# Channel mixer of a hybrid decoder layer on one core: the value sums and gelu's output are kept in PSUM, and the transposes of h are spread over the out projection

## The chip, the cores and the metric

The kernel runs on one core of a Trainium2 chip. The metric is the device time of one execution in microseconds (us). The engines are named as in the profile: PE is TensorE (PEld its weight loads), DVE is VectorE, ACT is ScalarE, POOL is GpSimd, SP is the queue that issues the DMAs. Each engine works through its own queue in order. SBUF is the on-chip memory that all engines read; PSUM is the accumulator memory that PE writes, eight banks of 512 fp32 for each of 128 partitions.

## The reference, cut to what matters

One decoder layer on x of 512 rows and 1024 columns. The change touches the second part of it only, from the out projection to the channel mixer:

```python
x = x + y @ w_out[i]
hf = rmsnorm(x, norm_ffn[i])
up = causal_dwconv(hf @ w_up[i], ffn_dw_w[i], ffn_dw_b[i])   # width 3, per channel
gate, val = jnp.split(up, 2, axis=-1)                        # 2816 channels each
x = x + (jax.nn.gelu(gate) * val) @ w_down[i]
```

Before it stand the conformer and attention mixers, behind it a gated per-layer embedding (`w_ple_gate`, `w_ple`) and a last norm.

## The kernel before, in words

**Numbers in two parts.** Every fp32 operand of a product is cut in two: a rounded high part, written by ACT (`hi_of`, L117), and the remainder, a subtraction (`lo_of`, L120) on DVE, for some blocks on POOL. A product is then three matmuls (high by high, high by low, low by high).

**Pairs.** The up projection and gelu run over 22 pairs f: 128 gate channels and the 128 value channels that belong to them. The rows are two halves of 256, the inner dimension two halves of 512, and each pair is made by a scheme of seven block products instead of eight (Strassen's kind). A product (`mm_block`, L133) is four inner blocks by three matmuls of 128x256, so a pair is 84 matmuls. They are called m1 to m7 and use sums of weight blocks: block 11 (m1, m2), t12 (m5, m6), t34 (m7, m4) and 22 (m3). Two PSUM banks take gates and two take values, in turn by f; LO and HI are a bank's halves. The products build on each other through ACT copies: m1 goes to an extra bank, is copied to the value bank's HI (L1322) and from there to the gate bank's LO (L1325); value HI is copied to value LO after m6 (L1336) and to gate HI after m7 (L1345); m5 is copied to SBUF (L1331).

**The stream of weights.** `Stream` (L218) keeps one list, `pieces`. A piece is loaded by SP, summed on POOL (an "add": two subtractions of 128x512, L307; "a" gives t12, "b" gives t34), or cut into hi and lo. `pump` cuts the next pieces as far as free buffers allow (four buffers `whl`; `done` frees one) and issues the next DMAs; `work` issues the pending lo part. For each pair DVE cuts 11, t12 and t34 (128x1024 each), POOL cuts 22 (128x512) and makes the four subtractions.

**The tail of a pair.** `after` (L1361) is a generator of steps: DVE adds m5 to the value bank into an SBUF tile v (L1366); ACT makes the middle tap and the bias of gate and value (L1371, L1373); DVE adds the other two taps (L1359: ug reads the gate bank, uv reads v); ACT makes gelu in SBUF (L1376); DVE multiplies (L1379); then hi and lo of the activations.

**The order.** It is written out by hand. `slot` (L1445) issues a product, the pending lo part, one step of each tail, then a pump. In the steady state the slots of a turn are m6, m2 of f, m1 of f+1, m7 of f, m5 of f+1, m3, m4 of f. After pairs 7 and 14 the down projection of the earlier pairs is put in (168 matmuls of 128x512), behind m1.

**The out projection** (`rows_product`, L1188 on) takes the row tiles t in the order 0, 2, 1, 3 in its second half. In the middle of a tile, after three of the four weight pieces (i == 2), `out_late` transposes the normed rows of the tile before: for tile 2 the sums s1, s2; for tile 1 its own halves and then s3, s4 and a22 of tile 2. `before_last` (L1412) does the norm of tile 3, the first half of the embedding's product, and m1 of pairs 0 and 1.

Of the kernel before, what the change touches and what calls it, by code (L numbers as in the profile page):

```python
# [12 lines left out]
AF = mybir.ActivationFunctionType  # L13
# [3 lines left out]
P = 128  # L17
# [66 lines left out]
def block_kernel(ctx: ExitStack, tc: tile.TileContext, x, p, rel_bias, norm_mix, w_in, conv_dw_w, conv_dw_b,  # L84
# [103 lines left out]
    def up_sums(*names):  # L188
        for name, f in names:
            pieces.append(((name, f), None, 4 if name == "22" else KC, P, "add" if name in ("a", "b") else "sum"))  # L190
# [4 lines left out]
    up_raw(0)  # L195
    up_sums(("a", 0), ("b", 0))
    up_raw(1)
    up_sums(("a", 1))
    ple_piece(0)
    up_sums(("11", 0), ("11", 1), ("t12", 0), ("t12", 1), ("b", 1), ("t34", 0), ("22", 0))  # L200
    for f in range(1, NF):
        if f + 1 < NF:
            up_raw(f + 1)
# [14 lines left out]
    class Stream:  # L218
# [133 lines left out]
        def done(self):  # L352
            self.hls -= 1
# [834 lines left out]
    def rows_product(name, ks, a_of, done, late=None, filler=None, between=None, last=None, banks=None, order=range(NT),  # L1188
                     cut_on=False):


        for n in range(2):
            o = [banks(n, t) if banks else ps() for t in range(NT)]

            def part(t, kk, hl):
                for j, k in enumerate(kk):
                    a_hi, a_lo = a_of(k, t)
                    mm_a(o[t], a_hi, a_lo, hl[:, 0, j, :], hl[:, 1, j, :], k == ks[0], k == ks[-1])

            hls = []  # L1200
            for i in range(0, len(ks), 2):
                kk = ks[i:i + 2]
                st.pump()
                hl = st.take(name, n, ks[i])
                hls.append((kk, hl))
                if n == 0 or late is None:
                    for t in range(NT):
                        part(t, kk, hl)
                        st.work()
                    st.done()  # L1210
            if n == 0 or late is None:
                for t in range(NT):
                    done(t, n, o[t])
                continue
            if between:
                between()
            before = None
            for t in order:
                if t == NT - 1 and last:
                    last(hls, o[t])  # L1220
                    break
                for i, (kk, hl) in enumerate(hls):
                    part(t, kk, hl)
                    st.work()
                    if t == NT - 1:
                        st.done()
                        if i < 2:
                            st.pump()
                    if cut_on and i == 2 and before is not None:
                        late(before)  # L1230
                done(t, n, o[t])
                if cut_on:
                    st.pump()
                elif before is not None:
                    late(before)
                before = t
            if filler:
                filler()
            if not last and not cut_on:
                late(NT - 1)  # L1240
# [30 lines left out]


    hf, hsum = {}, {}
    ROWS_FIRST, EVERY = ("s1", "s2"), ("s1", "s2", "s3", "s4", "a22")

    def row_sums(t):

# [35 lines left out]
    class Pair:  # L1313


        def __init__(self, f):
            self.f, self.gate, self.value, self.extra = f, gates[f % 2], values[f % 2], ps()

        def m1(self):
            self.b1 = st.take("11", self.f)  # L1320
            mm_block(self.extra[:, HI], self.b1, 0, hf["a11"], True)
            nc.scalar.activation(self.value[:, HI], self.extra[:, HI], AF.Copy)  # L1322

        def seed_gate(self):
            nc.scalar.activation(self.gate[:, LO], self.value[:, HI], AF.Copy)  # L1325

        def m5(self):
            self.t12 = st.take("t12", self.f)
            mm_block(self.extra[:, LO], self.t12, 0, hf["s1"], True)
            self.e = work("m5", (P, 256), tag="sc", bufs=2)  # L1330
            nc.scalar.activation(self.e, self.extra[:, LO], AF.Copy)  # L1331

        def m6(self):
            mm_block(self.value[:, HI], self.t12, 4, hf["s2"], False)
# [26 lines left out]
        def after(self):  # L1361

            f, c = self.f, NF + self.f
            uv, ug, v = [work(name, (P, 512), tag="S", bufs=8) for name in ("uv", "ug", "v")]
            halves = lambda a: a.rearrange("p (h t) -> p h t", h=2)
            nc.vector.tensor_tensor(halves(v), halves(self.value), self.e.unsqueeze(1).broadcast_to((P, 2, 256)),  # L1366
                                    op=ALU.add)
            yield
            yield
            yield  # L1370
            nc.scalar.activation(ug, self.gate, AF.Identity, scale=fw(2, f), bias=fw(3, f))  # L1371
            yield
            nc.scalar.activation(uv, v, AF.Identity, scale=fw(2, c), bias=fw(3, c))  # L1373
            self.taps(ug, self.gate, f)
            yield
            nc.scalar.activation(ug, ug, AF.Gelu_apprx_tanh)  # L1376
            self.taps(uv, v, c)
            yield
            nc.vector.tensor_tensor(uv, ug, uv, op=ALU.mult)  # L1379
            yield  # L1380
            a = act[f] = work("a", (P, 2, 512), F32R, tag="act", bufs=8)
            hi_of(a[:, 0], uv)
            yield
            yield
            yield
            lo_of(a[:, 1], uv, a[:, 0])
# [13 lines left out]
    def out_done(t, n, o):  # L1400
        residual(t, n, o, gain_f)
        if n and t != 3:
            ready(t)
        if n and t == 1:
            st.adds = 1

    def out_late(t):
        turn_halves(t, ROWS_FIRST if t == 2 else EVERY)
        if t == 1:
            turn_halves(2, ("s3", "s4", "a22"))  # L1410

    def before_last():  # L1412
        ready(3)
        st.adds = len(pieces)
        st.pump()
        ple_half(0)
        st.work()
        st.pump()
        pairs[0] = Pair(0)
        pairs[0].m1()  # L1420
        st.work()
        st.pump()
        turn_halves(3, ("s1",))
        pairs[0].seed_gate()
        pairs[1] = Pair(1)
        pairs[1].m1()
        st.work()
        st.pump()
        turn_halves(3, ("s2",))
        pairs[1].seed_gate()  # L1430

    rows_product("out", list(range(KC)),
# [9 lines left out]
            if next(tail, tails) is tails:  # L1442
                tails.remove(tail)

    def slot(product, cut=True):  # L1445

        product()
        st.work()
        step()
        if cut:  # L1450
            st.pump()

    def down(f0, f1, gain, *late, **kw):
        rows_product("down%d" % f0, list(range(f0, f1)),
# [7 lines left out]
    for f in range(NF):  # L1462
        this, coming = pairs[f], pairs.get(f + 1)
        if f == 0:
            slot(this.m5)
            turn_halves(3, ("s3",))
            slot(coming.m2)
            slot(this.m6)
            turn_halves(3, ("s4",))
            slot(coming.m5)  # L1470
            turn_halves(3, ("a22",))
            slot(this.m7)
            slot(this.m2)
        else:
            cut = f not in DOWN_IN
            slot(this.m6, cut)
            if f > 1:
                slot(this.m2, cut)
            else:
                step()  # L1480
            if f + 1 < NF:
                coming = pairs[f + 1] = Pair(f + 1)
                slot(coming.m1, cut)
            if f in DOWN_IN:
                step()
                st.pump(most=1)
                step()
                st.work()
                drain()
                down(*DOWN_IN[f], None, banks=lambda n, t: ps() if t < 3 else coming.gate)  # L1490
            slot(this.m7)
            if f + 1 < NF:
                slot(coming.m5)
                coming.seed_gate()
        tails.append(this.after())
        slot(this.m3)
        slot(this.m4)
    drain()
    gain_p = load_gain(norm_ple)
    hpT = [work("hpT", (P, 2, KC, P), F32R, tag="hf", bufs=7) for t in range(NT)]  # L1500
# [88 lines left out]
```

## Time and profile before

| | us |
|---|---|
| median of 3 runs (lowest, highest) | 855.8 (854.69, 857.84) |
| profiled execution, its own time | 857.31 |
| span of that execution | 855.3 |
| PE busy (share of the span) | 811.9 (95%) |
| DVE busy | 633.2 (74%) |
| ACT busy | 441.8 (52%) |
| POOL busy | 202.3 (24%) |

The span is the time from the first to the last recorded instruction; 2.0 us of the execution lie around it. Busy shares are means over stages with different limits. Matmuls overlap in the pipeline, so PE's pace is read from the distance of their starts and not from their durations. The out projection's second half and the pairs lie between 365 and 764 us of the span.

### The profile page before, as it was taken

How to read it: one execution, taken by the hardware profiler on the slowest of the kernel's cores; microseconds unless marked ns; L12 is line 12 of the kernel's file. 1: busy time of each engine (PE TensorE's matmuls, PEld its weight loads, DVE VectorE, ACT ScalarE, POOL GpSimd, SP SyncE). 2: the span in 40 equal slices, each digit the busy share in tenths (PEclk: the TensorE clock that was granted, in tenths of full speed). 3: DMA queues.
4: the chain of work that ended last, by engine and by line, in shares of the span. 5: the costliest groups of instructions: out<-in, count | busy, mean ns of one | idle time of the engine just before them, and what ended most of it. 6: DMA issues, size and time to landing. Idle time of an engine off the chain costs nothing.

```text
span 855.3 us, 12272 instructions
## 1 busy us (share of the span) xinstructions
PE 811.9 (95%) x4688; PEld 702.5 (82%) x4688; DVE 633.2 (74%) x965; ACT 441.8 (52%) x839; POOL 202.3 (24%) x183
## 2 busy tenths in 40 slices
PE   8999999999999999998898899998899998999996
PEld 6788888888888877876888898798887898888885
DVE  6479988888878879557698884388984388864664
ACT  6333434387779764335566653165662266642543
POOL 2000000000010000043585670147640256401012
PEclk9999999999999999999999999999999999999999
DMA  6347777221101122640233223313323332141322
GB/s 212 106 99 207 187 181 166 65 61 50 50 28 47 50 97 101 221 123 26 75 99 99 63 62 136 111 52 97 99 72 101 99 100 74 35 151 62 123 74 99
DMA packets 108070, 84.69 MB, mean 99 GB/s; under 512 B 4113, under 2 KB 93641, under 8 KB 108011
## 3 DMA queue, kind: packets, MB, share of 16 engines
q1 hardware_dynamic: 108010, 83.90, 33.6%
q8 instruction: 37, 0.61, 0.3%
q14 instruction: 23, 0.18, 0.1%
HBM read 79.36 MB, written 2.43 MB: 96 GB/s over the span
## 4 chain that ended last, share of the span: by engine, by line
PE 66%; DVE 24%; ACT 4%; issue 3%; POOL 1%; DMA 1%; SPq 0%; POOLq 0%; DVEq 0%; ACTq 0%
PE ps L128 9%; PE ps L130 9%; PE ps L129 8%; PE ps L142 8%; PE ps L141 8%; PE ps L143 8%; DVE whl L121 8%; DVE uv L1359 6%; DVE uv L1379 3%; ACT whl L118 3%; DVE ug L1359 3%; PE ps L869 2%; PE ps L895 2%; PE ps L675 2%; PE ps L137 1%
## 5 line engine op out<-in xcount | busy, mean ns | idle before, releaser
L121 DVE TENSOR_TENSOR whl<-wraw,whl 128x512 fp32r<-128x512 f32 (+1 forms) x140 | 130.6, 945 | 107.4 <-ACT whl L118 107.1
L137 PE MATMUL ps<-hf,whl 128*128 128x256 f32 x616 | 178.9, 290 | 12.0 <-DVE whl L121 11.3
L135 PE MATMUL ps<-hf,whl 128*128 128x256 f32 x616 | 178.4, 290 | 10.6 <-ACT whl L118 9.5
L136 PE MATMUL ps<-hf,whl 128*128 128x256 f32 x616 | 176.6, 287 | 2.0 <-DVE hf L121 2.0
L118 ACT ACTIVATE whl<-wraw 128x512 fp32r<-128x512 f32 (+1 forms) x160 | 123.5, 794 | 94.1 <-PE ps L143 43.0
L137 PEld LDWEIGHTS ps<-hf,whl 128*128 128x128 f32 x616 | 120.4, 195 | 16.1 <-DVE whl L121 15.2
L135 PEld LDWEIGHTS ps<-hf,whl 128*128 128x128 f32 x616 | 120.3, 195 | 13.3 <-ACT whl L118 11.8
L136 PEld LDWEIGHTS ps<-hf,whl 128*128 128x128 f32 x616 | 120.4, 195 | 2.3 <-DVE hf L121 2.2
L128 PE MATMUL ps<-hT,whl 128*128 128x512 f32 x256 | 101.9, 398 | 0.0
L130 PE MATMUL ps<-hT,whl 128*128 128x512 f32 x256 | 100.2, 391 | 0.3 <-DVE whl L121 0.3
L129 PE MATMUL ps<-hT,whl 128*128 128x512 f32 x256 | 99.9, 390 | 0.0
L735 DVE SCALAR_TENSOR_TENSOR acc<-aT,convw,acc 128x512 f32<-128x512 f32 x120 | 86.1, 745 | 1.0
L307 POOL TENSOR_TENSOR tt<-wraw 128x512 f32<-128x512 f32 x44 | 66.0, 1500 | 81.0 <-DVE whl L121 76.9
L307 POOL TENSOR_TENSOR tt<-wraw,tt 128x512 f32<-128x512 f32 x44 | 71.7, 1629 | 9.2 <-DVE whl L121 6.0
L121 DVE TENSOR_TENSOR whl<-tt,whl 128x1024 fp32r<-128x1024 f32 x44 | 54.9, 1278 | 23.1 <-ACT whl L118 23.1
L141 PE MATMUL ps<-whl,a 128*128 128x512 f32 x176 | 70.7, 402 | 0.6 <-DVE x L1256 0.6
L142 PE MATMUL ps<-whl,a 128*128 128x512 f32 x176 | 70.4, 400 | 0.0
L143 PE MATMUL ps<-whl,a 128*128 128x512 f32 x176 | 70.2, 399 | 0.0
L1359 DVE SCALAR_TENSOR_TENSOR uv<-v,ffnw,uv 128x511 f32<-128x511 f32 (+1 forms) x44 | 63.3, 1439 | 1.1 <-ACT uv L1373 0.3
L118 ACT ACTIVATE whl<-tt 128x1024 fp32r<-128x1024 f32 x44 | 46.0, 1046 | 22.4 <-PE ps L143 19.0
L130 PEld LDWEIGHTS ps<-hT,whl 128*128 128x128 f32 x256 | 48.1, 188 | 11.3 <-DVE whl L121 0.7
L128 PEld LDWEIGHTS ps<-hT,whl 128*128 128x128 f32 x256 | 48.1, 188 | 9.0 <-issue 0.2
(214 smaller groups left out, 1548.2 us busy)
## 6 DMA issues: line engine op xcount, KB each, us to landing
wraw<-in_w_up SPq DMA_DIRECT2D x44, 512.0 KB
wraw<-in_w_in SPq DMA_DIRECT2D x32, 512.0 KB
wraw<-in_w_down SPq DMA_DIRECT2D x20, 512.0 KB
wraw<-in_w_out SPq DMA_DIRECT2D x8, 512.0 KB
wraw<-in_w_ple_gate SPq DMA_DIRECT2D x8, 512.0 KB
W<-vdram SPq DMA_DIRECT2D x8, 264.0 KB
xin<-in_x SPq DMA_DIRECT2D x4, 512.0 KB
wraw<-in_w_ck SPq DMA_DIRECT2D x4, 512.0 KB
```

Source lines behind the costliest of these rows:

```text
L118: nc.scalar.activation(dst, src, AF.Copy, scale=scale)
L121: engine.tensor_tensor(dst, src, f32(hi), op=ALU.subtract)
L128: nc.tensor.matmul(o, hl[:, 0, j, cs], a_hi, start=start, stop=False)
L129: nc.tensor.matmul(o, hl[:, 0, j, cs], a_lo, start=False, stop=False)
L130: nc.tensor.matmul(o, hl[:, 1, j, cs], a_hi, start=False, stop=stop)
L135: nc.tensor.matmul(o, hl[:, 0, j0 + k, :], a[:, 0, k, :], start=start and k == 0, stop=False, skip_group_check=True)
L136: nc.tensor.matmul(o, hl[:, 0, j0 + k, :], a[:, 1, k, :], start=False, stop=False, skip_group_check=True)
L137: nc.tensor.matmul(o, hl[:, 1, j0 + k, :], a[:, 0, k, :], start=False, stop=k == 3, skip_group_check=True)
L141: nc.tensor.matmul(o, a_hi, w_hi, start=start, stop=False)
L142: nc.tensor.matmul(o, a_hi, w_lo, start=False, stop=False)
L143: nc.tensor.matmul(o, a_lo, w_hi, start=False, stop=stop)
L1359: nc.vector.scalar_tensor_tensor(u[:, d:], o[:, :S - d], fw(k, c), u[:, d:], op0=ALU.mult, op1=ALU.add)
```

## The change

Five things change. (1) The sum v is written back into the value bank, and both value taps and the ACT step read it there. (2) gelu's output goes to the gate bank and the product reads it there. (3) In the tail the value's ACT step and taps come before the gate's, and gelu and the product one step later each. (4) m1 and m5 take a PSUM bank each; the copies of m1 to the value and the gate bank move to the slots of m5 and m4 of the turn; m1 follows the down projection; a slot pumps before it steps the tails. (5) In the out projection the transposes are put at i == 2 or i == 3 by a table, the sum "a" of pair 1 comes later in `pieces`, and `before_last` pumps one piece only. The last down projection gets a pump and a `work` at the end of its first half.

```diff
-    up_sums(("a", 1))
     ple_piece(0)
-    up_sums(("11", 0), ("11", 1), ("t12", 0), ("t12", 1), ("b", 1), ("t34", 0), ("22", 0))
+    up_sums(("11", 0), ("11", 1), ("t12", 0), ("a", 1), ("t12", 1), ("b", 1), ("t34", 0), ("22", 0))
...
-                    if cut_on and i == 2 and before is not None:
-                        late(before)
+                    if cut_on and before is not None:
+                        late(before, i)
...
         def m1(self):
-            self.b1 = st.take("11", self.f)
-            mm_block(self.extra[:, HI], self.b1, 0, hf["a11"], True)
-            nc.scalar.activation(self.value[:, HI], self.extra[:, HI], AF.Copy)
+            self.first = ps()
+            self.b1 = self.b1 or st.take("11", self.f)
+            mm_block(self.first[:, LO], self.b1, 0, hf["a11"], True)
+
+        def seed_value(self):
+            nc.scalar.activation(self.value[:, HI], self.first[:, LO], AF.Copy)
 
         def seed_gate(self):
-            nc.scalar.activation(self.gate[:, LO], self.value[:, HI], AF.Copy)
+            nc.scalar.activation(self.gate[:, LO], self.first[:, LO], AF.Copy)
...
-            uv, ug, v = [work(name, (P, 512), tag="S", bufs=8) for name in ("uv", "ug", "v")]
+            uv, ug = [work(name, (P, 512), tag="S", bufs=8) for name in ("uv", "ug")]
+            v = self.value
...
+            nc.scalar.activation(uv, v, AF.Identity, scale=fw(2, c), bias=fw(3, c))
+            yield
             nc.scalar.activation(ug, self.gate, AF.Identity, scale=fw(2, f), bias=fw(3, f))
+            self.taps(uv, v, c)
             yield
-            nc.scalar.activation(uv, v, AF.Identity, scale=fw(2, c), bias=fw(3, c))
             self.taps(ug, self.gate, f)
             yield
-            nc.scalar.activation(ug, ug, AF.Gelu_apprx_tanh)
-            self.taps(uv, v, c)
+            nc.scalar.activation(self.gate, ug, AF.Gelu_apprx_tanh)
             yield
-            nc.vector.tensor_tensor(uv, ug, uv, op=ALU.mult)
+            nc.vector.tensor_tensor(uv, self.gate, uv, op=ALU.mult)
...
+    TURNS = {(0, 2): (0, ()), (2, 3): (2, ("s1", "s2")), (1, 2): (1, ()), (1, 3): (2, ("s3", "s4", "a22"))}
+
+    def out_late(t, i):
+        if (t, i) in TURNS:
+            turn_halves(*TURNS[t, i])
...
-    def slot(product, cut=True):
+    def slot(product, then=None, cut=True):
 
         product()
         st.work()
-        step()
+        if then:
+            then()
         if cut:
             st.pump()
+        step()
...
             if f + 1 < NF:
-                slot(coming.m5)
-                coming.seed_gate()
+                slot(coming.m5, coming.seed_value)
         tails.append(this.after())
         slot(this.m3)
-        slot(this.m4)
+        slot(this.m4, coming.seed_gate if 0 < f < NF - 1 else None)
```

## Rows read from the trace of the kernel before

**Rows 1.** The chain of waits between 597 and 635 us: shares of the stretch by engine and line, then one link of a turn (start us, length us, what).
```profile
by line: DVE whl L121 26.3%; DVE uv L1359 25.3%; DVE uv L1379 17.0%; DVE ug L1359 11.2%; ACT whl L118 11.1%; issue 7.7%; DVE a L121 4.8%; ACT a L118 0.5%; DVEq L1379 0.2%; ACTq L118 0.1%
...
609.80 1.05 ACT whl L118
```

**Rows 2.** VectorE's timeline: starts of the value sum v (L1366) at the turns that bound the stretches below.
```profile
425.36 0.68 DVE L1366 TENSOR_TENSOR v<-ps,m 128x512 f32<-128x512 f32 x1
...
450.12 0.68 DVE L1366 TENSOR_TENSOR v<-ps,m 128x512 f32<-128x512 f32 x1
...
510.67 0.68 DVE L1366 TENSOR_TENSOR v<-ps,m 128x512 f32<-128x512 f32 x1
...
560.90 0.69 DVE L1366 TENSOR_TENSOR v<-ps,m 128x512 f32<-128x512 f32 x1 [1.55 <-PE ps L137]
...
633.35 0.68 DVE L1366 TENSOR_TENSOR v<-ps,m 128x512 f32<-128x512 f32 x1
...
683.59 0.69 DVE L1366 TENSOR_TENSOR v<-ps,m 128x512 f32<-128x512 f32 x1 [1.54 <-PE ps L137]
...
731.82 0.68 DVE L1366 TENSOR_TENSOR v<-ps,m 128x512 f32<-128x512 f32 x1
```

**Rows 3.** VectorE's timeline: the rest of one turn (cuts, lo of a, taps uv, product; the taps ug stand between), and the taps and product of pair 14, beside which POOL has nothing.
```profile
598.75 1.23 DVE L121 TENSOR_TENSOR whl<-wraw,whl 128x1024 fp32r<-128x1024 f32 x1 [1.05 <-ACT whl L118]
599.90 2.35 DVE L121 TENSOR_TENSOR whl<-tt,whl 128x1024 fp32r<-128x1024 f32 x2
602.17 0.69 DVE L121 TENSOR_TENSOR a<-uv,a 128x512 fp32r<-128x512 f32 x1
...
604.21 3.30 DVE L1359 SCALAR_TENSOR_TENSOR uv<-v,ffnw,uv 128x511 f32<-128x511 f32 x2
607.62 1.60 DVE L1379 TENSOR_TENSOR uv<-ug,uv 128x512 f32<-128x512 f32 x1
...
639.40 1.53 DVE L1359 SCALAR_TENSOR_TENSOR uv<-v,ffnw,uv 128x511 f32<-128x511 f32 x2
641.04 0.69 DVE L1379 TENSOR_TENSOR uv<-ug,uv 128x512 f32<-128x512 f32 x1
```

**Rows 4.** GpSimd's timeline over the same turn: the lo of 22, the first and the last of the four subtractions.
```profile
602.18 1.83 POOL L121 TENSOR_TENSOR whl<-wraw,whl 128x512 fp32r<-128x512 f32 x1 [3.92 <-ACT whl L118]
603.97 1.29 POOL L307 TENSOR_TENSOR tt<-wraw 128x512 f32<-128x512 f32 x1
...
608.63 1.74 POOL L307 TENSOR_TENSOR tt<-wraw 128x512 f32<-128x512 f32 x1
```

**Rows 5.** The instructions of line L1359 over the whole span: count, shortest, median and longest in ns.
```profile
L1359 DVE SCALAR_TENSOR_TENSOR ug<-ps,ffnw,ug x44: 734/748/751, 429.8 to 755.6; 128x511 f32<-128x511 f32 x22, 128x510 f32<-128x510 f32 x22
L1359 DVE SCALAR_TENSOR_TENSOR uv<-v,ffnw,uv x44: 741/1608/1721, 431.3 to 757.6; 128x511 f32<-128x511 f32 x22, 128x510 f32<-128x510 f32 x22
```

**Rows 6.** TensorE's timeline: two matmuls of 128x256 that are 78 matmuls apart, one of the two waits of a steady turn, the longest wait of pair 2, two neighbours of 128x512.
```profile
588.14 0.28 PE L135 MATMUL ps<-hf,whl 128*128 128x256 f32 x1
...
597.50 0.28 PE L135 MATMUL ps<-hf,whl 128*128 128x256 f32 x1
...
587.92 0.39 PE L137 MATMUL ps<-hf,whl 128*128 128x256 f32 x1 [0.76 <-DVE whl L121]
...
451.86 0.38 PE L135 MATMUL ps<-hf,whl 128*128 128x256 f32 x1 [1.97 <-ACT whl L118]
...
534.40 0.39 PE L143 MATMUL ps<-whl,a 128*128 128x512 f32 x1
534.63 0.39 PE L141 MATMUL ps<-whl,a 128*128 128x512 f32 x1
```

**Rows 7.** ScalarE's timeline over one turn: hi of a, the copy after m6, hi of 22, the value's middle tap, gelu.
```profile
609.25 0.64 ACT L118 ACTIVATE a<-uv 128x512 fp32r<-128x512 f32 x1 [3.69 <-DVE uv L1379]
...
611.69 0.36 ACT L1336 ACTIVATE ps<-ps 128x256 f32<-128x256 f32 x1
...
613.60 0.62 ACT L118 ACTIVATE whl<-wraw 128x512 fp32r<-128x512 f32 x1
...
614.42 0.80 ACT L1373 ACTIVATE uv<-v,ffnw 128x512 f32<-128x512 f32 x1
...
616.66 0.63 ACT L1376 ACTIVATE ug<-ug 128x512 f32<-128x512 f32 x1
```

**Rows 8.** VectorE's timeline: the rows of tile 1 (L442), two cuts and one lo of a, each beside running POOL work.
```profile
391.92 3.44 DVE L442 SCALAR_TENSOR_TENSOR hhalf<-x,rstd,gain 128x512 f32<-128x512 f32 x2 [1.75 <-POOL rstd L433]
...
425.96 3.95 DVE L121 TENSOR_TENSOR whl<-tt,whl 128x1024 fp32r<-128x1024 f32 x2
...
441.94 1.78 DVE L121 TENSOR_TENSOR a<-uv,a 128x512 fp32r<-128x512 f32 x1
```

**Rows 9.** TensorE's timeline: the waits of the out projection's end and of pair 0.
```profile
386.66 1.38 PE L1299 MATMUL ps<-ci,hsum 128*128 128x128 f32 x8 [1.44 <-DVE hsum L1284]
...
395.51 0.63 PE L1299 MATMUL ps<-ci,hhalf 128*128 128x128 f32 x4 [1.05 <-DVE hhalf L442]
...
412.01 0.38 PE L136 MATMUL ps<-hf,whl 128*128 128x256 f32 x1 [1.98 <-DVE hf L121]
```

**Rows 10.** Stretches: PE, PEld, DVE, ACT and POOL busy us (instructions), TensorE's granted clock, DMA share, GB/s.
```profile
454.00:456.00 2.00, 2.00 (x11) 2.00 (x11) 2.00 (x4) 1.48 (x5) 0.73 (x1) 0.50 0.78 228
...
520.00:540.00 20.00, 19.70 (x85) 15.72 (x84) 9.02 (x11) 4.91 (x6) 0.00 (x0) 1.00 0.32 106
```

More of the change, by code (lines that the diff above doesn't have):

```diff
@@ L1211, in rows_product @@
             if n == 0 or late is None:
+                if late and name != "gate" and not cut_on:
+                    st.pump()
                 for t in range(NT):
                     done(t, n, o[t])
+                    if late and name != "gate" and not cut_on and t == 1:
+                        st.work()
                 continue
@@ L1273, in block_kernel @@
     hf, hsum = {}, {}
-    ROWS_FIRST, EVERY = ("s1", "s2"), ("s1", "s2", "s3", "s4", "a22")
+    EVERY = ("s1", "s2", "s3", "s4", "a22")
     def row_sums(t):
@@ L1316, in __init__ @@
         def __init__(self, f):
-            self.f, self.gate, self.value, self.extra = f, gates[f % 2], values[f % 2], ps()
+            self.f, self.gate, self.value = f, gates[f % 2], values[f % 2]
+            self.b1 = None
         def m1(self):
-            self.b1 = st.take("11", self.f)
-            mm_block(self.extra[:, HI], self.b1, 0, hf["a11"], True)
-            nc.scalar.activation(self.value[:, HI], self.extra[:, HI], AF.Copy)
+            self.first = ps()
[3 more added lines that the diff above has]
+            nc.scalar.activation(self.value[:, HI], self.first[:, LO], AF.Copy)
         def seed_gate(self):
-            nc.scalar.activation(self.gate[:, LO], self.value[:, HI], AF.Copy)
+            nc.scalar.activation(self.gate[:, LO], self.first[:, LO], AF.Copy)
         def m5(self):
             self.t12 = st.take("t12", self.f)
-            mm_block(self.extra[:, LO], self.t12, 0, hf["s1"], True)
-            self.e = work("m5", (P, 256), tag="sc", bufs=2)
-            nc.scalar.activation(self.e, self.extra[:, LO], AF.Copy)
+            o = ps()
+            mm_block(o[:, LO], self.t12, 0, hf["s1"], True)
+            self.m5_ = work("m5", (P, 256), tag="sc", bufs=2)
+            nc.scalar.activation(self.m5_, o[:, LO], AF.Copy)
         def m6(self):
@@ L1363, in after @@
             f, c = self.f, NF + self.f
-            uv, ug, v = [work(name, (P, 512), tag="S", bufs=8) for name in ("uv", "ug", "v")]
+            uv, ug = [work(name, (P, 512), tag="S", bufs=8) for name in ("uv", "ug")]
+            v = self.value
             halves = lambda a: a.rearrange("p (h t) -> p h t", h=2)
-            nc.vector.tensor_tensor(halves(v), halves(self.value), self.e.unsqueeze(1).broadcast_to((P, 2, 256)),
+            nc.vector.tensor_tensor(halves(v), halves(v), self.m5_.unsqueeze(1).broadcast_to((P, 2, 256)),
                                     op=ALU.add)
@@ L1382, in after @@
             hi_of(a[:, 0], uv)
-            yield
             yield
@@ L1403, in out_done @@
             ready(t)
[L1404 to L1410, printed above, removed]
+    TURNS = {(0, 2): (0, ()), (2, 3): (2, ("s1", "s2")), (1, 2): (1, ()), (1, 3): (2, ("s3", "s4", "a22"))}
+    def out_late(t, i):
+        if (t, i) in TURNS:
+            turn_halves(*TURNS[t, i])
     def before_last():
@@ L1414, in before_last @@
         st.adds = len(pieces)
-        st.pump()
+        st.pump(most=1)
         ple_half(0)
         st.work()
-        st.pump()
         pairs[0] = Pair(0)
@@ L1421, in before_last @@
         st.work()
-        st.pump()
         turn_halves(3, ("s1",))
+        pairs[0].seed_value()
         pairs[0].seed_gate()
@@ L1426, in before_last @@
         pairs[1].m1()
-        st.work()
-        st.pump()
         turn_halves(3, ("s2",))
+        pairs[1].seed_value()
         pairs[1].seed_gate()
@@ L1475, in block_kernel @@
             cut = f not in DOWN_IN
-            slot(this.m6, cut)
+            slot(this.m6, cut=cut)
             if f > 1:
-                slot(this.m2, cut)
+                slot(this.m2, cut=cut)
             else:
@@ L1482, in block_kernel @@
                 coming = pairs[f + 1] = Pair(f + 1)
-                slot(coming.m1, cut)
             if f in DOWN_IN:
+                coming.b1 = st.take("11", f + 1)
                 step()
@@ L1489, in block_kernel @@
                 drain()
-                down(*DOWN_IN[f], None, banks=lambda n, t: ps() if t < 3 else coming.gate)
+                down(*DOWN_IN[f], None)
+            if f + 1 < NF:
+                slot(coming.m1)
             slot(this.m7)
             if f + 1 < NF:
-                slot(coming.m5)
-                coming.seed_gate()
+                slot(coming.m5, coming.seed_value)
         tails.append(this.after())
         slot(this.m3)
-        slot(this.m4)
+        slot(this.m4, coming.seed_gate if 0 < f < NF - 1 else None)
     drain()
```

## The prediction, made before the result was known

> **What bounds the kernel now.** I read the page first: PE busy 95% of the span, DVE 74%. That looks like a kernel bound by PE, and in the pairs it isn't. The chain of waits between 597 and 635 us holds no PE at all: value taps 25.3%, weight cuts on DVE 26.3%, product 17.0%, gate taps 11.2%, cuts on ACT 11.1% [rows 1]. VectorE's timeline gives the pace. The sum v comes at 450.12 and 510.67 (five turns), 560.90 and 633.35 (six), 683.59 and 731.82 (four): 181.23 us for 15 turns, 12.08 each [rows 2]. PE needs less. Its 128x256 matmuls start 0.12 us apart (9.36 us for 78) [rows 6], so a pair of 84 is 10.08; the other 2.0 us are two waits, for ACT's and DVE's cut, 0.76 in the record and more in truth, since the ends of matmuls are modelled [rows 6].
>
> Why is DVE slow? Two value taps take 3.30 us in a steady turn and 1.53 for pair 14, beside which POOL is idle; the product takes 1.60 and 0.69 [rows 3]. In that turn POOL runs from 602.18 to 610.37 without a pause worth the name [rows 4], so it works beside both. The gate taps, which read one operand from PSUM, lie between 734 and 751 ns in all 44 cases; the value taps, both operands in SBUF, between 741 and 1721 [rows 5]. So DVE and POOL hinder each other where DVE reads two operands from SBUF, and POOL pays too: its subtraction is 1.29 or 1.74 us [rows 4]. [...]
>
> **The change part by part.**
>
> *v and gelu in PSUM (parts 1 and 2).* Each turn the taps fall from 3.30 to 1.53 and the product from 1.60 to 0.69: 2.7 us of DVE. Writing v into PSUM instead of SBUF is in no row for DVE. Bounds: at worst twice its 0.68 us, at best nothing changes; I take nothing, since ACT's 128x256 copy within PSUM takes 0.36 [rows 7], an ordinary length. gelu into PSUM likewise stays at 0.63 [rows 7]. [...]
>
> *The new order of the tail (part 3).* DVE's queue per turn: product, v, three cuts, lo of a, value taps, gate taps. As durations 0.69 + 0.68 + 1.23 + 2.35 + 0.69 + 1.53 + 1.53 = 8.7 [rows 2, 3]. New is that DVE has nothing between the gate taps and the product, so gelu's 0.63 [rows 7] stands in the ring: 9.3. POOL starts its five operations when ACT has cut 22, that is when DVE is at the third cut and the lo of a, and needs 5 x 1.29 = 6.5 us. Beside taps, gelu, product and v (1.53 + 1.53 + 0.63 + 0.69 + 0.68 = 5.1 us) it disturbs nobody, so some 1.4 us of it fall on cuts or on the lo of a; that lo took 1.78 instead of 0.69 beside POOL [rows 8], 1.1 more. DVE's ring is then 10.4 by durations and somewhat less by starts, since neighbours overlap slightly. PE's 10.08 is about the same. I take 10.3 per turn: 181.23 - 15 x 10.3 = **26.7 us**. Bounds: 10.08 (30.0 us) and, if all cuts meet POOL, the second rival.
>
> *Moved copies and pump before step (part 4).* In the ACT queue hi of a no longer stands ahead of the cut of 11: the link from the product's end to the cut at 609.80 [rows 1, 7] is gone. New waits: the copy to the gate bank waits for the product of the pair that had the bank, and behind it in ACT's queue stand the cut of t34, hi of a, the copy after m6, the cuts of t12 and 22, then the value's middle tap. The ring product, copy, three cuts and the rest, taps, gelu is 0.69 + 0.36 + 1.05 + 0.64 + 0.36 + 1.05 + 0.62 + 0.80 + 1.53 + 1.53 + 0.63 = 9.3 [rows 1, 3, 7], under 10.08: it costs nothing while the product comes in time. The copy to the value bank waits for the value taps, which come two slots before it; behind it stands gelu, which waits for the later gate taps anyway. Cover gone, each us of lateness is a us of PE. The GpSimd queue gets the same operations at the same slot; SP's DMAs (1 MB a turn) are issued as early as before.
>
> *Pairs 0 to 2.* From 425.36 to 450.12 two turns take 24.76 [rows 2]; at 10.3 they would be 20.6, 4.2 less. POOL is behind there and meets DVE's cuts (two in 3.95) [rows 8]. Bounds 0 and 4.6; I take **2.5**.
>
> *Around the down projections.* 510.67 to 560.90 and 633.35 to 683.59 take 50.2 each [rows 2]. PE's need is 10.08 + 168 x 0.23 = 48.7 [rows 6], 1.5 is lost. m1 is only moved behind it. Half of it goes, with the value taps: **1.5** for both; bounds 0 and 3.
>
> *Out projection and pair 0 (part 5).* PE waits 1.44 for s1 [rows 9]. At i == 3 the transposes stand behind six more matmuls, 6 x 0.23 = 1.4, which cover it. The rows of tile 1 take 3.44 for two [rows 8] beside the sum "a" of pair 1, which comes later now: about 1.53, as two undisturbed taps. That is 1.9 on a chain whose wait in PE is 1.05, and the last wait before m5 is 1.98 [rows 9]. Against it: with one pumped piece, t12 of pair 0 is cut only when m5 asks, 1.05 + 1.23 behind the copies, and "a" of pair 1 runs later. Bounds: 2.3 lost and 1.44 + 1.05 + 1.98 = 4.5 gained; I take **2.5**. The pump and `work` at the end of the last down projection's first half move a cut ahead of four additions; no PE wait stands there: nothing, within 0.7 either way, the length of one addition's place.
>
> *Sum.* 26.7 + 2.5 + 1.5 + 2.5 = 33.2. The profiled execution took 857.3 (span 855.3 and 2.0 around it), 1.5 more than the median of the three runs. 857.3 - 33.2 = 824.1; from the median 822.6. I say **823**.
>
> [...]
>
> **The rivals.**
>
> *The lock moves in part.* POOL's work meets half of the cuts instead of a fifth. Two cuts took 3.95 instead of 2.35, the lo of a 1.1 more [rows 8]: all four would be 3 x 0.8 + 1.1 = 3.5 a turn, half is 1.75. DVE's ring 9.3 + 1.75 = 11.05 saves 15 x 1.03 = 15.4, with half of the other terms 18.7: **838**. For it: POOL's start hangs on the cut of 22, close to DVE's own cuts. Against: 5.1 of 6.5 us find undisturbing company.
>
> *It moves wholly, and the kernel gets slower.* Place: DVE's queue from the product to the lo of a. If every cut and the lo of a meet POOL, the ring is 9.3 + 3.5 = 12.8, because gelu, formerly hidden beside the value taps, is now waited for. That is 0.7 x 15 = 10.8 longer, less the out projection's 2.5: about **865**. It decides from 12.08 - 9.3 = 2.8 us of contention a turn on. Against: four DVE instructions would have to be hit by 6.5 us of POOL that begins after the first two are done. [...]
>
> *The out projection gives back.* The late cut of t12 costs 2.3 instead of a gain of 2.5, with the turns as forecast: **828**.
>
> *It doesn't do what it says.* The length comes from something other than the operands' place, say from writing uv, and taps and product stay at 3.30 and 1.60: **856**, within 2. Against: the gate taps write the same kind of tile beside the same POOL work at 751 ns at most [rows 5].
>
> **How the numbers follow.** Forecast 65%, lock in part 15%, out projection gives back 9%, no effect 4%, slower 7%. The forecast's own range is 814 to 833: all bounds at their best give 30.0 + 4.6 + 3.0 + 4.5 = 42.1, 814; 10.7 a turn, with pairs 0 to 2 at nothing, gives 833. The range to 841 takes in the partial lock and the out projection's rival. What one measurement can tell from no change is 0.5%, 4.3 us. Faster: 65 + 15 + 9 = 89%; same 4%; slower 7%.
>
> **What would show it.** In the changed kernel: L1359's value taps with no case above 760 ns, a product of 0.69; v at distances of 10.1 to 10.5; the chain in these stretches mostly PE; DVE's idle time before the product released by gelu; cuts of 1.23 with a few longer ones, POOL's subtractions nearer 1.29. s1's wait gone. Wrong would be: turns of 11 or more with cuts above 1.6 (the lock has moved), PE waiting for the copies to gate or value bank, or an interval from 365 us to pair 0 that is longer than before.

## The result, and the profile after

The changed kernel took 828.7 us (median of four runs, 828.1 to 829.4) where the kernel before took 856.1 beside it (854.7 to 857.8): a ratio of 0.968, 95% interval 0.966 to 0.970. The gain is 27.4 us, the forecast was 33.2. The predicted 823 was 5.7 too low, inside the range.

The page of the changed kernel begins so (busy us, share of the span, instructions):

```profile
span 827.6 us, 12258 instructions
...
PE 802.1 (97%) x4688; PEld 695.1 (84%) x4688; DVE 606.1 (73%) x965; ACT 442.8 (54%) x839; POOL 190.4 (23%) x183
```

DVE is busy 27 us less. Starts of the sum v cut the span into stretches, as in [rows 2]. VectorE's timeline of the changed kernel:

```profile
424.00 0.69 DVE L1375 TENSOR_TENSOR ps<-ps,m 128x512 f32<-128x512 f32 x1
...
446.43 0.69 DVE L1375 TENSOR_TENSOR ps<-ps,m 128x512 f32<-128x512 f32 x1
...
499.13 0.69 DVE L1375 TENSOR_TENSOR ps<-ps,m 128x512 f32<-128x512 f32 x1
...
548.35 0.70 DVE L1375 TENSOR_TENSOR ps<-ps,m 128x512 f32<-128x512 f32 x1 [3.56 <-PE ps L137]
...
611.97 0.69 DVE L1375 TENSOR_TENSOR ps<-ps,m 128x512 f32<-128x512 f32 x1
...
661.21 0.70 DVE L1375 TENSOR_TENSOR ps<-ps,m 128x512 f32<-128x512 f32 x1 [3.55 <-PE ps L137]
...
703.75 0.69 DVE L1375 TENSOR_TENSOR ps<-ps,m 128x512 f32<-128x512 f32 x1
```

The first mark of the table is the first addition on cat, ahead of all changed code: 322.5 us before, 323.8 after, and 323.1 in a second execution of the changed kernel. So the two profiled executions simply differ there by 1.3.

| stretch (us of the two profiled spans) | before | after | gain | forecast |
|---|---|---|---|---|
| start to the first addition on cat | 322.5 | 323.8 | -1.3 | 0 |
| to the first v: out projection, pair 0 | 102.8 | 100.2 | 2.6 | 2.5 |
| two turns of pairs 0 to 2 | 24.8 | 22.4 | 2.3 | 2.5 |
| 15 turns | 181.2 | 158.9 | 22.4 | 26.7 |
| around the two down projections | 100.5 | 98.5 | 2.0 | 1.5 |
| the last v of these to the end | 123.5 | 123.9 | -0.4 | 0 |
| span | 855.3 | 827.6 | 27.7 | 33.2 |

A turn is 10.59 us on the mean and 10.54 when steady, where the prediction took 10.3 and PE needs 10.08. The instructions that the change was about are these (line by line over the whole span: shortest, median and longest in ns), to be held against [rows 5]:

```profile
L1367 DVE SCALAR_TENSOR_TENSOR uv<-ps,ffnw,uv x44: 736/748/753, 428.5 to 729.2; 128x511 f32<-128x511 f32 x22, 128x510 f32<-128x510 f32 x22
...
L1389 DVE TENSOR_TENSOR uv<-ps,uv x22: 684/692/694, 433.4 to 732.7; 128x512 f32<-128x512 f32 x22
...
L1375 DVE TENSOR_TENSOR ps<-ps,m x22: 689/690/699, 424.0 to 723.0; 128x512 f32<-128x512 f32 x22
...
L121 DVE TENSOR_TENSOR a<-uv,a x22: 678/1785/1792, 440.4 to 734.1; 128x512 fp32r<-128x512 f32 x22
```

All 44 value taps and all 22 products are short. The lo of a is the new long one: 1785 ns in the median, once 0.69 [rows 3]. Now one turn in its order, first VectorE's timeline (start, length, and in brackets the idle time before it and what ended it):

```profile
579.75 0.69 DVE L1389 TENSOR_TENSOR uv<-ps,uv 128x512 f32<-128x512 f32 x1 [0.73 <-ACT ps L1387]
...
580.95 1.43 DVE L121 TENSOR_TENSOR whl<-wraw,whl 128x1024 fp32r<-128x1024 f32 x1
...
583.74 1.23 DVE L121 TENSOR_TENSOR whl<-tt,whl 128x1024 fp32r<-128x1024 f32 x1 [0.22 <-ACT whl L118]
584.88 1.78 DVE L121 TENSOR_TENSOR a<-uv,a 128x512 fp32r<-128x512 f32 x1
586.59 1.52 DVE L1367 SCALAR_TENSOR_TENSOR uv<-ps,ffnw,uv 128x511 f32<-128x511 f32 x2
588.03 1.52 DVE L1367 SCALAR_TENSOR_TENSOR ug<-ps,ffnw,ug 128x511 f32<-128x511 f32 x2
```

then ScalarE's of the same turn:

```profile
579.11 0.60 ACT L1387 ACTIVATE ps<-ug 128x512 f32<-128x512 f32 x1 [1.07 <-DVE ug L1367]
579.65 1.05 ACT L118 ACTIVATE whl<-wraw 128x1024 fp32r<-128x1024 f32 x1
580.60 0.36 ACT L1332 ACTIVATE ps<-ps 128x256 f32<-128x256 f32 x1
580.90 1.04 ACT L118 ACTIVATE whl<-tt 128x1024 fp32r<-128x1024 f32 x1
581.85 0.61 ACT L118 ACTIVATE a<-uv 128x512 fp32r<-128x512 f32 x1
582.37 0.36 ACT L1344 ACTIVATE ps<-ps 128x256 f32<-128x256 f32 x1
582.67 1.04 ACT L118 ACTIVATE whl<-tt 128x1024 fp32r<-128x1024 f32 x1
...
589.65 0.60 ACT L1387 ACTIVATE ps<-ug 128x512 f32<-128x512 f32 x1 [1.07 <-DVE ug L1367]
```

and GpSimd's:

```profile
580.00 1.30 POOL L306 TENSOR_TENSOR tt<-wraw 128x512 f32<-128x512 f32 x1
584.30 1.81 POOL L121 TENSOR_TENSOR whl<-wraw,whl 128x512 fp32r<-128x512 f32 x1 [3.00 <-ACT whl L118]
```

Read as one chain, this is a closed ring: gelu 579.11, then in ACT's queue the cut of 11 (579.65), the copy to the gate bank (580.60), the cut of t34, hi of a, the copy after m6 and the cut of t12 (582.67); DVE's third cut, which waits for that one (583.74); lo of a, beside POOL's lo of 22 (584.30); value taps, gate taps, and the next gelu at 589.65. That is 10.54 us, start to start. The product (579.75) is no link of it. The copy to the gate bank needs the product, but that ends at 580.44, while ACT is still at the cut of 11. In the run below with gelu in SBUF, where the copy doesn't need the product, it starts just as late behind gelu: 1.49 us in both.

The rows also show who pays when DVE and POOL meet: the one that begins second, and about for as long as the first still runs. POOL's lo of 22 begins during the third cut; the cut keeps its 1.23 and POOL's operation takes 1.81, where the shortest of its kind takes 1.28. The lo of a begins with 1.23 us of that operation left and takes 1.1 longer. The cut of 11 (580.95) begins with 0.35 us left of a subtraction and takes 0.2 longer.

The chain of waits between 565 and 612 us says the same by its shares, and still holds no PE:

```profile
by line: ACT whl L118 22.5%; DVE a L121 18.1%; DVE ug L1367 15.2%; DVE uv L1367 15.1%; issue 10.6%; DVE whl L121 10.4%; ACT a L118 3.7%; ACT ps L1344 2.5%; ACT ps L1332 2.1%; ACT ps L1387 1.8%; DVE ps L1375 0.9%; ACTq L1387 0.2%; DVE uv L13
```

Against [rows 1], the product is gone from the chain, and the lo of a stands in it with 18.1% where it had 4.8%.

### The profile page after: what moved, and what is told of

Read it like the earlier page. It is cut to its first block, busy times and chain, and to the rows that moved or that the text cites. A ratio compares the mean times of both kernels' runs of the same rounds, so it can differ in the third digit from the quotient of the medians.

```text
span 827.6 us, 12258 instructions
## 1 busy us (share of the span) xinstructions
PE 802.1 (97%) x4688; PEld 695.1 (84%) x4688; DVE 606.1 (73%) x965; ACT 442.8 (54%) x839; POOL 190.4 (23%) x183
## 4 chain that ended last, share of the span: by engine, by line
PE 68%; DVE 16%; ACT 9%; issue 3%; POOL 2%; DMA 1%; SPq 0%; POOLq 0%; ACTq 0%; DVEq 0%
PE ps L128 9%; PE ps L130 9%; PE ps L129 9%; PE ps L142 8%; PE ps L143 8%; PE ps L141 8%; ACT whl L118 5%; DVE whl L121 5%; DVE a L121 3%; DVE ug L1367 3%; DVE uv L1367 3%; PE ps L868 2%; PE ps L894 2%; PE ps L135 2%; PE ps L137 2%
## 5 line engine op out<-in xcount | busy, mean ns | idle before, releaser
L121 DVE TENSOR_TENSOR whl<-wraw,whl 128x512 fp32r<-128x512 f32 (+1 forms) x140 | 133.7, 968 | 84.0 <-ACT whl L118 80.5
L135 PE MATMUL ps<-hf,whl 128*128 128x256 f32 x616 | 176.3, 286 | 4.7 <-ACT ps L1332 2.4
L137 PE MATMUL ps<-hf,whl 128*128 128x256 f32 x616 | 174.7, 284 | 2.3 <-DVE whl L121 1.8
L136 PE MATMUL ps<-hf,whl 128*128 128x256 f32 x616 | 174.2, 283 | 0.0
L135 PEld LDWEIGHTS ps<-hf,whl 128*128 128x128 f32 x616 | 118.0, 192 | 8.5 <-ACT ps L1332 4.8
L137 PEld LDWEIGHTS ps<-hf,whl 128*128 128x128 f32 x616 | 118.1, 192 | 3.2 <-DVE whl L121 2.5
L136 PEld LDWEIGHTS ps<-hf,whl 128*128 128x128 f32 x616 | 118.1, 192 | 0.0
L130 PE MATMUL ps<-hT,whl 128*128 128x512 f32 x256 | 100.2, 391 | 0.3 <-DVE whl L121 0.3
L121 DVE TENSOR_TENSOR whl<-tt,whl 128x1024 fp32r<-128x1024 f32 x44 | 58.5, 1334 | 24.4 <-ACT whl L118 23.8
L142 PE MATMUL ps<-whl,a 128*128 128x512 f32 x176 | 69.6, 396 | 1.2 <-DVE whl L121 1.2
L141 PE MATMUL ps<-whl,a 128*128 128x512 f32 x176 | 69.7, 396 | 0.7 <-DVE x L1259 0.7
L143 PE MATMUL ps<-whl,a 128*128 128x512 f32 x176 | 69.4, 395 | 0.0
L306 POOL TENSOR_TENSOR tt<-wraw,tt 128x512 f32<-128x512 f32 x44 | 60.0, 1364 | 9.3 <-DVE whl L121 6.0
L130 PEld LDWEIGHTS ps<-hT,whl 128*128 128x128 f32 x256 | 48.0, 188 | 11.2 <-DVE whl L121 0.7
L128 PEld LDWEIGHTS ps<-hT,whl 128*128 128x128 f32 x256 | 48.1, 188 | 9.0 <-issue 0.2
L129 PEld LDWEIGHTS ps<-hT,whl 128*128 128x128 f32 x256 | 48.2, 188 | 8.7
```

What stands on the lines that cost most here:

```text
L121: engine.tensor_tensor(dst, src, f32(hi), op=ALU.subtract)
L128: nc.tensor.matmul(o, hl[:, 0, j, cs], a_hi, start=start, stop=False)
L129: nc.tensor.matmul(o, hl[:, 0, j, cs], a_lo, start=False, stop=False)
L130: nc.tensor.matmul(o, hl[:, 1, j, cs], a_hi, start=False, stop=stop)
L141: nc.tensor.matmul(o, a_hi, w_hi, start=start, stop=False)
L142: nc.tensor.matmul(o, a_hi, w_lo, start=False, stop=False)
```

## The experiments

Two theories stood against each other. Mine: the operands' place did it, by ending the meetings of DVE and POOL. The rival: the new order of the tail and of the copies did it. Diffs are against the changed kernel unless another is named. A time from a single run has no interval; there I lean on the turns, which agree within a few hundredths.

**v in SBUF again.**

```diff
-            uv, ug = [work(name, (P, 512), tag="S", bufs=8) for name in ("uv", "ug")]
-            v = self.value
+            uv, ug, v = [work(name, (P, 512), tag="S", bufs=8) for name in ("uv", "ug", "v")]
...
-            nc.vector.tensor_tensor(halves(v), halves(v), ...
+            nc.vector.tensor_tensor(halves(v), halves(self.value), ...
```

> The changed kernel with the sum v in an SBUF tile again; gelu and the product stay in PSUM, the new order stays. Theory (DVE and POOL hinder each other where DVE reads two SBUF operands): POOL works beside the value taps, so they take about 1.65 us each instead of 0.75, a turn grows from 10.54 to about 12.3, and the time to 855 to 860 us. Rival (the new order of tail and copies brought the gain, the bank of the operand did not): taps and turn stay within 0.3 us of the changed kernel, 829 to 834 us.

Measured: 859.6 us in one run (before, beside it: 856.9). The line of the value taps over its span:

```profile
L1367 DVE SCALAR_TENSOR_TENSOR uv<-v,ffnw,uv x44: 737/1668/1784, 429.0 to 759.1; 128x511 f32<-128x511 f32 x22, 128x510 f32<-128x510 f32 x22
```

The taps are back at 1.67 us, two of them take 3.47 instead of 1.52 in a steady turn, and the turn is 12.50: the ring of 10.54 plus 1.95. The whole gain goes with this one operand.

**gelu in SBUF again**, v in PSUM.

```diff
-            nc.scalar.activation(self.gate, ug, AF.Gelu_apprx_tanh)
+            nc.scalar.activation(ug, ug, AF.Gelu_apprx_tanh)
...
-            nc.vector.tensor_tensor(uv, self.gate, uv, op=ALU.mult)
+            nc.vector.tensor_tensor(uv, ug, uv, op=ALU.mult)
```

> The changed kernel with gelu's output in SBUF again, so that the product reads two SBUF operands; v stays in PSUM. Theory: the product meets POOL's last two subtractions and takes 1.3 to 1.6 us instead of 0.69, but it is not in the ring that sets the turn (gelu, ACT's three cuts, DVE's third cut, lo of a, taps), so a turn grows by 0 to 0.4 us and the time is 829 to 836 us. Rival (product's place in DVE's queue sets the turn): turn 11.4, 841 to 845 us.

Measured: 832.9 us, steady turn 10.67. The product:

```profile
L1389 DVE TENSOR_TENSOR uv<-ug,uv x22: 684/811/1312, 434.1 to 736.3; 128x512 f32<-128x512 f32 x22
```

A median of 0.81, not the 1.3 to 1.6 expected: in the new order the product begins when POOL is just ending its third subtraction. The cut of 11 pays too, 1.70 instead of 1.43. So the 0.9 us a turn that the prediction booked for the product was mostly the order's to give, and gelu's place is worth 0.13 a turn.

**Both in SBUF**, so only the order is new (both edits above).

> The changed kernel with v and gelu's output both in SBUF again: the new order alone. Theory (the operands' place brings the gain, the order only makes room for it): value taps 1.67 us, product 0.7 to 1.3, turn 12.4 to 12.8, time 859 to 864 us, a little slower than the kernel before, because gelu no longer lies beside the value taps. Rival (the order has a gain of its own): below 852 us.

Measured: 860.2 us (before, beside it: 858.4), turn 12.5, value taps 739/1666/1784 ns. The order alone gives nothing. That is the end of the rival as it was put. Not run is the counterpart, the old order with both operands in PSUM, so how much of the gain needs the new order beside them stays open.

**The kernel before, with POOL's subtractions replaced by fills.** No data is read by them.

```diff
-            sub = lambda to, x_, y_: nc.gpsimd.tensor_tensor(to, x_, y_, op=ALU.subtract)
+            sub = lambda to, x_, y_: nc.gpsimd.memset(to, 0.0)
```

> The kernel before, with POOL's four subtractions per pair replaced by fills of the same tiles with zero, which read nothing (this leaves the weight sums out). Theory (POOL's reads of SBUF hinder DVE): value taps 0.75 and product 0.69 in the steady turns, turn 10.1 to 10.6 instead of 12.1, time 822 to 831 us. Rival A (any POOL work hinders DVE): taps stay above 1.2 us and the time above 840 us. Rival B (the taps are slow for where v and uv lie in SBUF, whatever POOL does): taps stay at 1.6, 855 us.

Measured: 819.6 us, below what was expected, with turns of 10.08, PE's own pace. VectorE's timeline of it:

```profile
580.13 1.53 DVE L1359 SCALAR_TENSOR_TENSOR uv<-v,ffnw,uv 128x511 f32<-128x511 f32 x2
```

and GpSimd's at that moment:

```profile
579.87 1.92 POOL L307 MEMSET tt<- 128x512 f32 x4
```

Two value taps with v in SBUF take 1.53 us right beside four fills. Taps and POOL work side by side, and nothing is lost while POOL reads nothing. A caveat: a fill is 0.48 us and a subtraction 1.29, so POOL also works less here. The tap's place, POOL's reading and the length of the tap are tied together by this and the three runs above.

**The changed kernel with the same fills.**

> The changed kernel with POOL's four subtractions per pair replaced by zero fills (this leaves the weight sums out). POOL's lo of 22 stays and still meets the lo of a. Theory (the changed kernel's turn of 10.54 holds 1.1 us of contention between these two, the subtractions are not in it): lo of a stays at 1.7 to 1.8, turn 10.5, time 825 to 829 us. Rival (the subtractions set the turn): turn 10.1, 819 to 822 us.

Measured: 824.0 us, 1 below the time expected, and steady turns of exactly 10.54 again, with the lo of a at 1.78 beside POOL's lo of 22 (which stays a subtraction) and the cut of 11 back at 1.22. So the four subtractions cost the changed kernel's steady turn nothing; of the meetings, only that of lo of 22 with lo of a lies in its ring. The lower time comes from the beginning: the first v is at 421.0 instead of 424.0, and the first two turns take 20.2 us instead of 22.4.

**The lo of a one step earlier**, four runs. One `yield` less between hi and lo of a, so that DVE does it ahead of the third cut.

> The changed kernel with one yield less between hi and lo of the activations, so that lo of a stands before DVE's third cut and not beside POOL's lo of 22. Theory (the turn of 10.54 is the ring gelu, ACT's cuts, DVE's third cut, lo of a at 1.79 instead of 0.69, taps): lo of a 0.7, turn 10.1, PE's own pace, time 820 to 824 us. Rival (the ring is ACT's queue with the copy to the gate bank, and lo of a has slack): turn 10.5, 828 to 830 us.

Measured: 825.5 us (825.0 to 826.1), ratio 0.963 (0.960 to 0.967), between the two ranges expected. The lo of a falls to 0.68 and the 15 turns together stay at 158.9 us, with single turns from 9.2 to 12.6; the gain lies in the first two turns (19.1 us). VectorE's timeline shows where the meeting went:

```profile
578.49 2.37 DVE L121 TENSOR_TENSOR whl<-wraw,whl 128x1024 fp32r<-128x1024 f32 x1
...
581.92 0.68 DVE L121 TENSOR_TENSOR a<-uv,a 128x512 fp32r<-128x512 f32 x1
582.52 2.31 DVE L121 TENSOR_TENSOR whl<-tt,whl 128x1024 fp32r<-128x1024 f32 x1
```

and GpSimd's:

```profile
578.48 1.30 POOL L306 TENSOR_TENSOR tt<-wraw 128x512 f32<-128x512 f32 x1
...
582.37 1.38 POOL L121 TENSOR_TENSOR whl<-wraw,whl 128x512 fp32r<-128x512 f32 x1 [2.60 <-ACT whl L118]
```

Both long cuts begin within 0.2 us of a POOL operation and take 1.1 us too much. Moved, not removed: what the first rival called the lock, DVE and POOL holding each other up, at other instructions. The turns expected to fall to 10.1 did not.

**That, and the cut of 22 later**, four runs. In the slots of m2 the pieces of the tail go ahead of the pumped cut, so ACT cuts 22 after the value's middle tap and POOL begins later.

```diff
-            yield
...
-    def slot(product, then=None, cut=True):
+    def slot(product, then=None, cut=True, early=False):
...
+        if early:
+            step()
...
-        step()
+        if not early:
+            step()
...
-                slot(this.m2, cut=cut)
+                slot(this.m2, cut=cut, early=True)
```

> The kernel with the early lo of a (825.5 us), and in the m2 slots the tails step before the pump, so that ACT cuts 22 after the value's middle tap and POOL begins 0.7 us later, when DVE's third cut already runs. Theory (the turns that still take over 11 us are those in which POOL's lo of 22 starts just ahead of DVE's third cut, 2.31 instead of 1.23): all turns near 10.1, 820 to 823 us. Rival (those turns come from POOL's last subtraction meeting the cut of 11): no gain or a loss, 825 to 828 us.

Measured: 823.9 us (823.0 to 824.4), ratio 0.960 (0.958 to 0.962): 0.9 above the range expected, and below the changed kernel's 827.5 to 829.4 in eight runs. The 15 turns take 153.1 us, 10.21 each. One cut still meets POOL:

```profile
578.80 2.08 DVE L121 TENSOR_TENSOR whl<-tt,whl 128x1024 fp32r<-128x1024 f32 x1 [0.16 <-ACT whl L118]
580.80 0.68 DVE L121 TENSOR_TENSOR a<-uv,a 128x512 fp32r<-128x512 f32 x1
```

But the ring no longer sets the pace alone: the chain of waits between 565 and 612 us, which held no PE in the changed kernel, now holds it with 42%.

```profile
by line: DVE whl L121 19.0%; PE ps L137 14.3%; PE ps L135 14.0%; PE ps L136 14.0%; issue 13.6%; DVE ug L1367 6.1%; DVE uv L1367 6.0%; ACT ps L1387 3.9%; DVE ps L1375 3.8%; DVE a L121 2.9%; PE ps L142 1.1%; ACT ps L1329 0.8%; DVE uv L1389 0.
```

**The slot in its old order**, the step ahead of the pump, one run.

> The changed kernel with the old order within a slot, tails stepped before the pump. Theory (the ring of 10.54 runs through ACT's cuts and the contended lo of a): ACT takes the value's middle tap ahead of the cut of 22, POOL's lo of 22 then begins after DVE's lo of a has begun or later, lo of a falls to 0.7 in most turns and the turn to 10.1 to 10.4; but hi of a and gelu now stand ahead of cuts. 822 to 829 us. Rival (pump before step is what made the turn short): turn above 10.8, above 832 us.

Measured: 826.2 us; steady turns go 9.44 and 11.33 by turns, 10.40 on the mean of the 15, with the lo of a at 0.68 and 1.78 in the same beat. "Pump before step" is not what made turns short; by this one run it costs 0.2.

**The transposes of h as before (part 5 undone, but for the pump and `work` in the last down projection)**, four runs; its core:

```diff
-    TURNS = {(0, 2): (0, ()), (2, 3): (2, ("s1", "s2")), (1, 2): (1, ()), (1, 3): (2, ("s3", "s4", "a22"))}
+    TURNS = {(0, 2): (0, ()), (2, 2): (2, ("s1", "s2")), (1, 2): (1, ())}
...
-        st.pump(most=1)
+        st.pump()
```

> The changed kernel with part 5 undone in the out projection: transposes all at i == 2, the sum a of pair 1 before the embedding's piece, all pumps of before_last back. Theory (part 5 is worth the 2.6 us by which the first v stands earlier, once the later start of the whole trace is taken off): PE's wait of 1.4 for s1 and the long rows of tile 1 come back, 830.5 to 832.5 us. Rival (part 5 only shifts waits, and the gain there comes from pairs 0 and 1): 828 to 829.5 us.

Measured: 832.6 us (831.3 to 833.9), ratio 0.970 (0.968 to 0.972). The time is at the upper edge of the theory's range, but the interval of the ratio overlaps the changed kernel's, so the ratios alone don't settle it. The trace does: from the first addition on cat to the first v it takes 104.5 us, against 100.2 in the changed kernel (101.0 in a second execution) and 102.8 before. Its waits in TensorE's timeline are those of [rows 9]:

```profile
388.12 1.38 PE L1303 MATMUL ps<-ci,hsum 128*128 128x128 f32 x8 [1.42 <-DVE hsum L1288]
...
413.49 0.39 PE L136 MATMUL ps<-hf,whl 128*128 128x256 f32 x1 [1.98 <-DVE hf L121]
```

So part 5 is worth 3.6 to 4.3 us with the other parts in place, 1.7 of which make up for what those lose there. The changed kernel has other waits in their place:

```profile
406.60 0.63 PE L1302 MATMUL ps<-ci,hsum 128*128 128x128 f32 x4 [1.24 <-DVE hsum L1287]
...
415.83 0.39 PE L137 MATMUL ps<-hf,whl 128*128 128x256 f32 x1 [1.30 <-DVE whl L121]
```

**One more pump behind the embedding's product**, on top of the best kernel, to bring the cut of t12 of pair 1 forward; five runs.

```diff
+        st.pump()
```

> The kernel with the early lo of a and the later cut of 22, and one more pump in before_last behind the embedding's product, so that POOL makes the sum a of pair 1 before the sums of h's rows. Theory (PE's waits of 1.24 for s1 and 1.3 for the cut of t12 of pair 1 are one budget of POOL and DVE): the second wait goes, but s3 stands behind the sum a in POOL's queue and the rows of tile 3 meet it, so the first grows by 1 to 2 us; first v within 1 us of the kernel without that pump, time within 0.2% of it. Rival (POOL has room there): first v 1.3 us earlier.

Measured: 830.4 us (829.9 to 831.9), ratio 0.967 (0.966 to 0.969) where the kernel it started from has 0.960, 6.5 us worse; a miss for both expectations. The wait for that cut is gone and a longer one stands there. TensorE's timeline:

```profile
413.17 0.58 PE L135 MATMUL ps<-hf,whl 128*128 128x256 f32 x1 [5.08 <-ACT ps L1332]
```

and ScalarE's:

```profile
411.03 1.06 ACT L118 ACTIVATE whl<-tt 128x1024 fp32r<-128x1024 f32 x1 [6.97 <-POOL tt L306]
```

The cut was put into ACT's queue ahead of the copies that PE needs, and it waits 6.97 us for a sum that POOL makes late.

**The changed kernel once more**, four runs beside the last one and the old slot order.

> The changed kernel itself, once more, as the measure beside the next kernel on the same chip: ratio to the kernel before 0.966 to 0.970 by every theory.

Measured: 827.9 us (827.5 to 828.4), ratio 0.964 (0.962 to 0.966), lower than expected since the kernel before took 859.3 beside it and 856.1 in the first comparison. The changed kernel itself moved by 0.8. Its steady turns are 10.54 again, but its first two take 20.6 us, not 22.4: that stretch differs by 1.8 from one execution to the next.

## Why the prediction was right, and where it was not

*What bounds the kernel: right.* DVE was the bound of the pairs, through two SBUF operands beside POOL work. Taking v back to SBUF loses all of the gain (859.6 us); taking POOL's reads away in the kernel before brings the turn to 10.08, PE's pace as worked out from [rows 6].

*v and gelu in PSUM: right in kind.* Taps 1.52 for two and product 0.69 as forecast, the write of v 690 ns against 0.68 [rows 2], gelu 0.60 against 0.63 [rows 7]: the "nothing" booked for both writes holds. Reading v from PSUM costs the taps nothing either: their median is 748 ns with v in PSUM and 749 with v in SBUF where POOL only fills. Beside POOL's subtractions, v in SBUF took 31 us more (859.6 against 828.7). Mis-sized was the product's share, as the run with gelu in SBUF shows.

*The new order of the tail: the step that failed.* "I take 10.3 per turn" should have been 10.54. The 4.3 us between 26.7 and 22.4 are this term, and most of the miss. DVE's own ring came out as reckoned: 10.54 less its wait of 0.22 for the third cut's input is 10.32, with 1.1 more for the lo of a, as forecast, and 0.2 for the cut of 11, which was not. So DVE's ring as such wasn't the limit. What failed is the other ring of the prediction, the one through ACT's queue, put at 9.3, under PE's 10.08, so that it "costs nothing while the product comes in time". It had three links wrong. It went from gelu to the copy by the product (0.69), where ACT's cut of 11 (1.05) is the longer way. And it went from ACT's cut of t12 to the taps by the cut of 22 and the middle tap (0.62 + 0.80), where DVE's third cut and the lo of a (1.23 + 1.78) are. That is 2.0 more, 11.2 by durations; neighbours overlap, and by starts it is 10.54. What I had not put together is the one ring that changes from ACT's queue to DVE's.

*Moved copies: not quite nothing.* The copy to the gate bank is a link of the ring, and PE waits some 0.2 us for it in a steady turn; between 449 and 500 us these are PE's only waits. PE waiting for that copy was named as a sign of being wrong. From TensorE's timeline of the changed kernel:

```profile
489.26 0.39 PE L135 MATMUL ps<-hf,whl 128*128 128x256 f32 x1 [0.20 <-ACT ps L1332]
```

*Pairs 0 to 2, the down projections, out projection: right in size* (2.3 for 2.5, 2.0 for 1.5, 2.6 for 2.5). For the first, the second execution would have given 4.2. In the out projection the ways differ from the text: s1's wait went, as forecast, the rows of tile 1 fell from 3.44 [rows 8] to 1.41, but the late cut of t12 did cost 1.30, at pair 1 and not at pair 0, and the sum s1 of the next tile 1.24. The rival there was half right, and smaller: that the term came out near 2.5 is in part luck.

*Pair 19 to the end: nearly nothing, as forecast, but by two differences not foreseen that cancel.* Its first turn is 10.54 instead of 9.42: in the kernel before POOL's last subtraction ends early in that turn, while the new ring has its length whatever POOL subtracts. The next turn is 8.72 instead of 9.73.

*Rivals.* The partial lock has its place in the result: the steady turn holds 1.3 us of meetings on DVE (1.1 for the lo of a, 0.2 for the cut of 11), between the forecast's 1.1 and its 1.75. The lock in whole and "no effect" did not come; the run with only the order new is what the second would have looked like.

*What the signs said.* Taps, product, gelu's 0.73 before the product and the missing s1 wait came as named; turns of 10.54 lie just over the 10.1 to 10.5 given; "the chain mostly PE" was wrong, and that sign tells that a ring still set the pace. The granted clock rose from 0.94 in the mean of the stretch to 1.00; 0.50 and 1.00 are the two levels in [rows 10] (windows: sum busy of PE, PEld, DVE, ACT, POOL, clock, DMA share, GB/s). Before, five turns from 450 us on:

```profile
450.00:510.00 60.00, 53.67 (x408) 52.25 (x409) 53.90 (x51) 37.44 (x65) 38.30 (x24) 0.94 0.28 80
```

After, 49 us from the same mark on:

```profile
450.00:499.00 49.00, 48.17 (x395) 47.36 (x395) 44.06 (x47) 34.14 (x60) 35.77 (x25) 1.00 0.33 96
```

The 1.8 us by which the first two turns differ between the two executions of the changed kernel lie in the second turn (12.37 and 10.53). They come with a late DMA: the subtraction that POOL begins ahead of the first v waits for weights until 421.67 us, 2.3 ahead of that v, in the longer one, and until 420.43, 3.7 ahead of it, in the other. In the longer one two cuts of the second turn then meet POOL (4.55 us for two, from 435.96 on; 1.21 and 1.23 in the other).

Still open: why that DMA landed later, and why the medians of the kernel before go from 856.1 to 859.3 between groups of runs; within a group its runs lie 3 to 5 us apart.

## What to carry to other kernels

Where VectorE and GpSimd work side by side, look for VectorE instructions that come in two lengths, and give one operand of those on the critical ring a place in PSUM: here two value taps took 3.30 us in a steady turn with v in SBUF and 1.52 with v in PSUM. Look for the ring across queues (whose copy does the next engine's queue stand behind?) before summing one engine's load: here neither DVE's nor ACT's own ring was the limit, but the one that changes from ACT to DVE. And when one meeting is removed by moving an instruction, find which instruction is met instead; it took the moved cut of 22 as well to bring the turn from 10.54 to 10.2.

## What was not expected of the hardware

- GpSimd's fills, which only write, left VectorE's two-SBUF taps at 739 to 753 ns, so GpSimd's being busy is not enough to slow them.
- The price of a meeting for VectorE's cuts and lo of a didn't depend on the length of the instruction, but on how much of GpSimd's is left when it begins. With 1.2 us or more left it is about 1.1: 0.68 to 1.78 us for the lo of a, 1.21 to 2.31 for a cut. With 0.35 left it is 0.2, and with nothing running at the start it is nothing: the 70 cuts and lo of a that begin so between 425 and 760 us of the changed kernel are within 0.02 us of the shortest of their size. GpSimd pays in the same way when it begins second: its subtractions go from 1.29 to as much as 2.29, when a cut still has 1.12 to 1.13 to run.
- In a steady turn the meetings settle: the same instruction meets the same one turn after turn (10.53 to 10.55 us), or in a beat of two turns (9.44 and 11.33).
